# A decoder layer's MLP rows and last product: another order, the sums of w_down at another place, other tile sizes

## The chip, the cores and the metric

The kernel runs on one core of one Trainium2 chip. The metric is the device time in microseconds from the first to the last instruction of one execution, with what lies around it. Five engines work side by side, each on a queue of its own in a fixed order: PE (matmuls), ACT and DVE (elementwise work), POOL (a little elementwise work, and the issue of transfers), SP (the issue of transfers only). All transfers, whichever queue issues them, are carried out by the same 16 DMA engines.

## The reference

One decoder layer on 1024 tokens of width 1024, all in float32:

```python
n = rms_norm(h, ln_mix_g);  proj = n @ w_in
ya = dilated_mixture(qa, ka, va) @ w_branch_a        # 12 heads, three dilations
yb = stick_breaking(qb, kb, vb) @ w_branch_b         # 8 heads, causal
h  = h + (sigmoid(ga) * ya + sigmoid(gb) * yb) @ w_out
h  = h + memory_cross_attn(rms_norm(h), rms_norm(mem), ...)
u  = rms_norm(h, ln_ffn_g) @ w_up                    # 1024 -> 2 * 2816
u  = depthwise_conv(u, conv_w, width=3) + conv_b
h  = h + (silu(gate) * val) @ w_down                 # 2816 -> 1024
return rms_norm(h, ln_f_g)
```

What matters below are the last three lines: w_up with the convolution and the gate, w_down, and the final norm.

## The kernel before

**Products.** A float32 operand is split into a high part and the remainder (`split_to`, L82 on ACT and L83 on DVE), and every product is three matmuls of 128 x 512, high by high, high by low, low by high (`mm3`, L99 to L101).

**w_up.** The 44 column blocks of w_up are handled as 22 rows g, a gate block and a value block at a time. A row is a fast 2 x 2 block product: seven block products instead of eight, on sums of weight halves (`sum_weights`) and sums of activation halves (the tiles t2, t3, t4 of `right_sums`). A row accumulates in two PSUM banks. Bank A takes the product p1, then s2·t2 (copied out as U2, L948), then s1·t1 (copied out as U4, L953), then s4·22 (copied to ug, L958). Bank B takes s3·t3 (copied to uv, L917; an accumulating DMA from POOL adds U4 to it, L918) and then l22·t4 (copied to uv, and another accumulating DMA adds U2). Then ACT and DVE do the convolution of ug and uv (L966 to L968), Silu and the product (L970, L973), and POOL stores the result and its block sums to `r_d` in DRAM (L976 to L990). Row g+1 starts (`up_start`) ahead of the end of row g (`up_end`), and its middle (`up_middle`) behind it.

**Early rows.** For the rows g below NEARLY = 10 two of the seven products (p1 and the one that goes to ug) are made earlier, beside the cross attention (`up_early`), and parked in DRAM. p1 is parked as two halves phi and plo in `er_d`. In the row both halves are read back by DMAs from POOL's queue and put into bank A by two matmuls with the identity `ident_r` (L906, L907).

**w_down.** `down` makes seven products (`run`), each over 11 steps kg, one left operand for each product: four are blocks of w_down itself, three are sums of its blocks. These sums (`weight_sums`) are made in DRAM, in `sd_d`, without any engine: for each of the 11 kg, four plain DMAs from SP ("puts", L519, 256 KB each) and three accumulating DMAs from POOL ("adds", L522, one of 512 KB and two of 256 KB), each of which waits for the one before. `sum_step` issues what is due of them. It is called in the loop over the attention's units once p has reached the stick-breaking pairs, and eight times in the merge after it. Each call issues the next operation of every second sum or so.

**The end.** The last product's four tiles end together in the last kg. `into` adds them to h and squares them, and only then `out_half` scales the four tiles and stores them (L1035 to L1039). The loads of h for the first product (`load_h`) are issued at kg 3 to 6.

**Order and memory.** A scheduler fixes one order for each engine when the program is built. DMAs of the sums and of h keep their order in the code. SBUF tiles lie in pools that are stacked from the left and from the right. By the sizes of the tiles the left pools' rows begin at 128 bytes beyond a multiple of 256, those of most right pools (attention, cross attention, t2 to t4, w_down) at a multiple of 256.

## Time and profile before

| | us |
|---|---|
| three runs | 1784.14, 1780.95, 1777.82 |
| median | 1780.95 |
| profiled execution, whole | 1780.45 |
| profiled execution, span of the trace | 1778.6 |
| PE busy | 1693.4 (95%) |
| DVE busy | 1113.0 (63%) |
| ACT busy | 871.0 (49%) |
| POOL busy | 326.9 (18%) |

The stages in the span: projections to about 100 us, dilated attention to 400, stick-breaking attention to 740, merge to 822, w_out and cross attention to 1108, the early products and the sums of the activations to 1150, the 22 rows of w_up to 1530, the first product of w_down to 1585, six more of 30 us each, and a tail of 13 us behind the last matmul. A stage is read from its own rows: PE is busy nearly everywhere, so what counts is where it waits, and for whom.

### The profile page before, as it was taken

The page shows a single profiled execution, that of the slowest core. Times are in us where ns is not written, and L with a number is a line of the kernel's source. Part 1 is how long each engine was busy: PE and PEld are TensorE (multiplying, and loading weights), DVE is VectorE, ACT ScalarE, POOL GpSimd, SP SyncE. Part 2 cuts the span into 40 slices and gives each one's busy share as a digit, 9 for nine tenths or more (in the row PEclk, how much of TensorE's full clock was granted, in tenths as well). Part 3 has the DMA queues.
Part 4 walks back from the last instruction along what each step waited for, and adds up shares of the span by engine and source line. Part 5 has one row for each costly group of instructions (what it writes and reads, how often), then busy time and mean ns, then how long its engine had stood idle before and what let it go on. Part 6 is the DMA issues. An engine that isn't in the chain of part 4 may idle for free.

```text
span 1778.6 us, 23614 instructions
## 1 busy us (share of the span) xinstructions
PE 1693.4 (95%) x8598; PEld 1378.1 (77%) x8598; DVE 1113.0 (63%) x1737; ACT 871.0 (49%) x1495; POOL 326.9 (18%) x511
## 2 busy tenths in 40 slices
PE   7999999998999899999999989798999999989997
PEld 5977777878878787788888767576778888778885
DVE  3764654468757466575645666777777767655556
ACT  5344544466345445444534455454555555534344
POOL 0442333221112110001000102222222222200002
PEclk9999999999999999999999999899999999999999
DMA  7443333455774843566322325666755454677664
GB/s 305 113 123 92 107 83 84 134 134 145 200 140 118 159 113 95 180 181 249 131 95 72 130 83 178 206 165 184 211 148 157 136 136 125 188 259 231 214 191 140
DMA packets 106388, 273.01 MB, mean 153 GB/s; under 512 B 16096, under 2 KB 16352, under 8 KB 106272
## 3 DMA queue, kind: packets, MB, share of 16 engines
q1 hardware_dynamic: 66368, 166.68, 28.9%
q0 software_dynamic: 39904, 104.82, 24.1%
q8 instruction: 68, 1.11, 0.3%
q14 instruction: 48, 0.39, 0.1%
HBM read 188.77 MB, written 74.29 MB: 148 GB/s over the span
## 4 chain that ended last, share of the span: by engine, by line
PE 66%; issue 13%; DMA 10%; DVE 5%; ACT 3%; POOL 3%; SPq 0%; POOLq 0%; DVEq 0%; ACTq 0%
PE mm L99 4%; PE mm L101 4%; PE mm L100 4%; PE pA L99 3%; PE pA L100 3%; PE pA L101 3%; DMA sd_d<-in_w_down_dram 2%; DMA uv<-U 2%; PE mmt L99 2%; PE dA L100 2%; PE dA L101 2%; PE mmt L100 2%; PE mmt L101 2%; PE dA L99 2%; DMA xw<-xs 2%
## 5 line engine op out<-in xcount | busy, mean ns | idle before, releaser
L101 PE MATMUL mm<-a2h,wl 128*128 128x512 f32 x592 | 235.2, 398 | 0.0
L99 PE MATMUL mm<-a2h,wh 128*128 128x512 f32 x592 | 234.7, 396 | 0.0
L100 PE MATMUL mm<-a2l,wh 128*128 128x512 f32 x592 | 234.5, 396 | 0.0
L83 DVE TENSOR_TENSOR wl<-wr,wh 128x1024 fp32r<-128x1024 f32 (+1 forms) x119 | 145.3, 1222 | 95.0 <-ACT wh L82 92.1
L82 ACT ACTIVATE wh<-wr 128x1024 fp32r<-128x1024 f32 (+1 forms) x119 | 124.0, 1043 | 132.6 <-PE mmt L101 29.2
L83 DVE TENSOR_TENSOR dl<-rl,dh 128x1024 fp32r<-128x1024 f32 x77 | 94.1, 1224 | 85.0 <-ACT dh L82 81.5
L82 ACT ACTIVATE dh<-rl 128x1024 fp32r<-128x1024 f32 x77 | 81.2, 1058 | 114.6 <-PE dA L101 41.2
L101 PEld LDWEIGHTS mm<-a2h,wl 128*128 128x128 f32 x592 | 112.4, 190 | 22.2 <-issue 1.0
L100 PEld LDWEIGHTS mm<-a2l,wh 128*128 128x128 f32 x592 | 112.3, 190 | 22.3 <-issue 0.9
L99 PEld LDWEIGHTS mm<-a2h,wh 128*128 128x128 f32 x592 | 112.5, 190 | 22.0 <-issue 0.9
L493 DVE TENSOR_TENSOR_SCAN kp<-kp 128x128 f32<-128x128 f32 (+7 forms) x64 | 86.8, 1356 | 29.4 <-ACT kp L490 29.1
L99 PE MATMUL pA<-a2h,mh 128*128 128x512 f32 x176 | 70.5, 400 | 14.9 <-ACT U L953 14.9
L502 ACT ACTIVATE at<-tra 128x512 f32<-128x512 f32 (+3 forms) x96 | 43.3, 489 | 76.9 <-PE tra L500 59.6
L112 POOL TENSOR_TENSOR ss<-ss,neghalf 128x1 f32<-128x1 f32 x24 | 23.3, 995 | 307.6 <-DVE ss L597 305.7
L490 ACT ACTIVATE kp<-zz,zsc 128x512 f32<-128x512 f32 (+3 forms) x96 | 55.6, 583 | 49.3 <-DVE zz L489 44.5
L381 ACT ACTIVATE sp<-sp,nm 128x128 f32<-128x128 f32 (+1 forms) x96 | 42.3, 442 | 72.6 <-DVE nm L379 72.5
L100 PE MATMUL dA<-dl,dh 128*128 128x512 f32 x176 | 70.1, 398 | 3.5 <-DVE dl L83 3.5
L101 PE MATMUL dA<-dh,dl 128*128 128x512 f32 x176 | 70.0, 397 | 0.0
L101 PE MATMUL pA<-a2h,ml 128*128 128x512 f32 x176 | 69.3, 394 | 0.0
L100 PE MATMUL pA<-a2l,mh 128*128 128x512 f32 x176 | 69.3, 394 | 0.0
L99 PE MATMUL dA<-dh 128*128 128x512 f32 x176 | 62.1, 393 | 3.8 <-ACT dh L82 3.8
L491 ACT ACTIVATE gg<-zz,zsc 128x512 f32<-128x512 f32 (+3 forms) x96 | 55.7, 583 | 7.1 <-DVE gg L494 7.1
(352 smaller groups left out, 4587.4 us busy)
## 6 DMA issues: line engine op xcount, KB each, us to landing
rl<-r_d SPq DMA_DIRECT2D x77, 256.0 KB, 3.2
wr<-in_w_in_dram SPq DMA_DIRECT2D x37, 512.0 KB, 4.2
wr<-in_w_up_dram SPq DMA_DIRECT2D x32, 512.0 KB, 4.3
w<-in_w_up_dram SPq DMA_DIRECT2D x22, 512.0 KB, 3.7
uv<-U POOLq DMA_DIRECT2D x44, 256.0 KB, 4.7
r_d<-ts POOLq DMA_DIRECT2D x44, 256.0 KB, 4.8
rl<-sd_d SPq DMA_DIRECT2D x44, 256.0 KB, 3.6
r_d<-y POOLq DMA_DIRECT2D x33, 256.0 KB, 3.4
```

Of the source, the lines that this page charges most:

```text
L82: nc.scalar.activation(hi, raw, AF.Copy)
L83: nc.vector.tensor_tensor(lo, raw, f(hi), op=ALU.subtract)
L99: nc.tensor.matmul(ps, wh, rh, start=first, stop=False, **kw)
L100: nc.tensor.matmul(ps, wh, ro, start=False, stop=False, **kw)
L101: nc.tensor.matmul(ps, wo, rh, start=False, stop=last, **kw)
L112: nc.gpsimd.tensor_tensor(ss, ss, neghalf[:, :n], op=ALU.pow)
L381: nc.scalar.activation(sp[:, a, :n], sp[:, a, :n], AF.Exp, scale=0.125, bias=nm[:, a:a + 1], accum_out=ost[:, 130 + a:131 + a])
L490: nc.scalar.activation(kp[:, c0:c1], z[:, :n], AF.Sigmoid, scale=zsc[:, 1, i:i + 1])
L491: nc.scalar.activation(gg[:, c0:c1], z[:, :n], AF.Sigmoid, scale=zsc[:, 0, i:i + 1])
L493: nc.vector.tensor_tensor_scan(rev, rev, rev, 1.0, op0=ALU.mult, op1=ALU.bypass)
L502: nc.scalar.activation(s[:, :nb * P], tp[:, :nb * P], AF.Copy)
```

## The change

Six things change.

1. In the rows below 9 `up_end` writes l22·t4 ahead of s4·22.
2. p1 is parked as one float32 tile, stored from POOL, read back by SP, and put into bank A by one float32 matmul with `ident`. The subtraction that made plo, `er_d` and `ident_r` are gone.
3. Four tiles get other sizes, so that all pools begin at 128 bytes beyond a multiple of 256.
4. The sums of w_down leave the attention and the merge. `sum_step` is called twice in each row from g = 6 on, a sum's six operations follow each other step by step, and a new sum begins every second step. So from row 8 to row 16 one row issues four puts and three adds.
5. The loads of h stand at kg 6 to 9.
6. In the last product the last four kg are made tile by tile, and each tile is scaled and stored as soon as it is added.

```diff
-            if p >= NA:
-                sum_step()
...
-        sum_step()
...
     def sum_step():
-            d = n - 3 * b
-            if 0 <= d < 12 and d % 2 == 0:
-                ops[d // 2]()
+            d = n - 2 * b
+            if 0 <= d < 6:
+                ops[d]()
...
-    neghalf = cp.tile([P, 16], F32, name="neghalf")
-    ident_r = cp.tile([P, P + 16], F32R, name="ident_r")[:, :P]
+    neghalf = cp.tile([P, 32], F32, name="neghalf")
-    rs8 = ap.tile([P, 16], F32, name="rs8")[:, 0:8]
+    rs8 = ap.tile([P, 48], F32, name="rs8")[:, 0:8]
-        rsm = xp.tile([P, 18], F32, name="rsm")[:, :2]
+        rsm = xp.tile([P, 50], F32, name="rsm")[:, :2]
-    ncw = mp.tile([P, 160], F32, name="ncw")
+    ncw = mp.tile([P, 192], F32, name="ncw")
...
     def up_early(gs):
-            hi, lo = etile("phi", F32R), etile("plo", F32R)
-            hilo(hi, lo, ps[g][0])
-            nc.gpsimd.dma_start(er_d[g, 0], hi)
-            nc.gpsimd.dma_start(er_d[g, 1], lo)
+            p1 = etile("p1")
+            nc.scalar.activation(p1, ps[g][0], AF.Copy)
+            nc.gpsimd.dma_start(e_d[g, 0], p1)
...
     def up_start(g):
-            nc.gpsimd.dma_start(hi, er_d[g, 0])
-            nc.gpsimd.dma_start(lo, er_d[g, 1])
-            nc.tensor.matmul(u["A"], ident_r, hi, start=True, stop=False, skip_group_check=True)
-            nc.tensor.matmul(u["A"], ident_r, lo, start=False, stop=True, skip_group_check=True)
+            p1 = etile("p1")
+            nc.sync.dma_start(p1, e_d[g, 0])
+            nc.tensor.matmul(u["A"], ident, p1, start=True, stop=True, skip_group_check=True)
...
     def up_middle(g, u):
+        if g >= 6:
+            sum_step()
     def up_end(g, u):
+        if g >= 6:
+            sum_step()
+        for part in (c21, c12) if g + 1 < NEARLY else (c12, c21):
+            part()
...
     def run(ps, i, first, also=(), ends=0):
-                if kg >= 3 and kg - 3 < len(also):
-                    tc.keep_in_program_order(also[kg - 3]())
+                if kg >= 6 and kg - 6 < len(also):
+                    tc.keep_in_program_order(also[kg - 6]())
...
+            ws = [(kg, *operands(i, kg)) for kg in range(KG - ends, KG)]
+            for t in range(4 if ends else 0):
+                for w in ws:
+                    step(t, *w)
     def into(ps, th, ch, op, last=None):
+                if last:
+                    out_tile(4 * th + t)
...
-        out_half(0)
-        run(A, 3, False)
+        run(A, 3, False, ends=4)
         into(A, 1, 0, ALU.add, 1)
-        out_half(1)
```

`operands` is the loads and the split of one kg, `step` the three matmuls of one tile, and `out_tile` the body of the loop of `out_half`; they are taken out of their functions unchanged.

PE's order is nearly the same up to the early products. Of the places where orders differ, these follow. In the names, mh and ml hold the two halves of a pair of weight sums, wh and wl those of a weight block, a2h and a2l those of the activations.

PE before, row 1 of w_up: the last three matmuls of s1·t1 in bank A, and behind them the first three of s4·22 in the same bank.

```order
L99 MATMUL pA_10261<-a2h_9759,mh_10321 128x512
L100 MATMUL pA_10261<-a2l_9760,mh_10321 128x512
L101 MATMUL pA_10261<-a2h_9759,ml_10322 128x512
L99 MATMUL pA_10261<-a2h_9759,mh_10325 128x512
L100 MATMUL pA_10261<-a2l_9760,mh_10325 128x512
L101 MATMUL pA_10261<-a2h_9759,ml_10326 128x512
```

After, PE in the same row: behind the last three of s1·t1 stand the matmuls of l22·t4 in bank B, twelve in all.

```order
L97 MATMUL pA_10148<-a2h_9673,mh_10205 128x512
L98 MATMUL pA_10148<-a2l_9674,mh_10205 128x512
L99 MATMUL pA_10148<-a2h_9673,ml_10206 128x512
L97 MATMUL pB_10227<-t4h_10036,wh_10197 128x512
L98 MATMUL pB_10227<-t4l_10037,wh_10197 128x512
L99 MATMUL pB_10227<-t4h_10036,wl_10198 128x512
```

So twelve matmuls now stand between the two products of bank A. It is the same in rows 0, 2, 3 and 6. In row 4 of after (and in rows 5, 7 and 8) PE still has both products back to back, and l22·t4 comes after the next row has begun.

```order
L99 MATMUL pA_10491<-a2h_9673,ml_10562 128x512
L97 MATMUL pA_10491<-a2h_9673,mh_10561 128x512
L98 MATMUL pA_10491<-a2l_9674,mh_10561 128x512
L99 MATMUL pA_10491<-a2h_9673,ml_10562 128x512
L97 MATMUL pA_10491<-a2h_9673,mh_10565 128x512
L98 MATMUL pA_10491<-a2l_9674,mh_10565 128x512
L99 MATMUL pA_10491<-a2h_9673,ml_10566 128x512
```

The first of s4·22 is the last line there: nothing moved. In rows 11 and 13, which had 22 and 20 matmuls between the two products, there is none left after.

POOL before, a late row (U2, U4 and p1 are added to uv and ug; ts and y go to `r_d`): the additions of U4 and U2 stand one behind the other.

```order
L938 MEMSET uv_11911 128x2
L918 DMA ug_11910<-p1_11933 128x512
L980 DMA r_d_75<-y_11967 128x512
L981 DMA r_d_75<-y_11967 128x512
L986 DMA r_d_75<-ts_11975 128x512
L988 DMA r_d_75<-ts_11976 128x512
L990 DMA r_d_75<-ts_11977 128x512
L918 DMA uv_11911<-U4_12058 128x512
L918 DMA uv_11911<-U2_12031 128x512
```

POOL after, a late row: behind the addition of U4 stand the three adds of the sums, then two stores, then the addition of U2.

```order
L931 MEMSET uv_11977 128x2
L909 DMA uv_11977<-U4_12118 128x512
L519 DMA sd_d_73<-in_w_down_dram 128x512 x2
L519 DMA sd_d_73<-in_w_down_dram 128x1024
L977 DMA r_d_74<-y_12036 128x512
L985 DMA r_d_74<-ts_12189 128x512
L909 DMA uv_11977<-U2_12091 128x512
L931 MEMSET ug_12122 128x2
L909 DMA ug_12122<-p1_12145 128x512
```

The adds moved in between the two additions to uv, on the queue that carries both.

SP before, late rows: only the loads of the weights.

```order
L901 DMA w2_12358<-in_w_up_dram 128x1024
L72 DMA wr_12204<-in_w_up_dram 128x1024
L901 DMA w2_12497<-in_w_up_dram 128x1024
L72 DMA wr_12356<-in_w_up_dram 128x1024
L901 DMA w2_12649<-in_w_up_dram 128x1024
```

SP after, late rows: the same loads with four puts for each row among them.

```order
L894 DMA w2_12430<-in_w_up_dram 128x1024
L516 DMA sd_d_73<-sd_d_73 128x512
L516 DMA sd_d_73<-in_w_down_dram 128x512 x2
L70 DMA wr_12284<-in_w_up_dram 128x1024
L894 DMA w2_12585<-in_w_up_dram 128x1024
L516 DMA sd_d_73<-sd_d_73 128x512 x2
L516 DMA sd_d_73<-in_w_down_dram 128x512 x2
L70 DMA wr_12428<-in_w_up_dram 128x1024
L516 DMA sd_d_73<-sd_d_73 128x512
L894 DMA w2_12725<-in_w_up_dram 128x1024
```

The puts moved in ahead of the weights of the rows to come, and those that read `sd_d` wait for the adds.

## Rows read from the trace of the kernel before

**Rows 1.** page, part 1: busy us (share of the span) xinstructions

```profile
PE 1693.4 (95%) x8598; PEld 1378.1 (77%) x8598; DVE 1113.0 (63%) x1737; ACT 871.0 (49%) x1495; POOL 326.9 (18%) x511
```

**Rows 2.** busy time by stage of the end, columns in the first line

```profile
core 0: us, PE busy (x) PEld busy (x) DVE busy (x) ACT busy (x) POOL busy (x), PEclk, DMA share, GB/s
1108.00:1150.00 42.00, 32.09 (x123) 24.48 (x122) 34.70 (x38) 21.53 (x28) 10.38 (x21) 0.87 0.69 213
1173.00:1253.00 80.00, 70.57 (x295) 55.78 (x294) 61.11 (x67) 41.99 (x55) 24.57 (x48) 0.98 0.69 199
1309.30:1463.70 154.40, 154.40 (x672) 125.97 (x671) 117.12 (x122) 86.46 (x113) 37.34 (x68) 1.00 0.53 142
1530.00:1586.00 56.00, 48.65 (x198) 38.10 (x196) 32.96 (x32) 25.25 (x28) 7.19 (x13) 0.94 0.81 258
```

**Rows 3.** timeline of PE, row 1 and row 3: start, us, instruction, [idle before]

```profile
1174.89 0.50 PE L99 MATMUL pA<-a2h,mh 128*128 128x512 f32 x1 [1.41 <-ACT U L953]
...
1207.55 0.50 PE L99 MATMUL pA<-a2h,mh 128*128 128x512 f32 x1 [2.05 <-ACT U L953]
```

**Rows 4.** waits: who waited for whom: us in total, times, longest

```profile
PE pA L99 <- ACT U L953: 14.9, 8, 3.2
...
SPq L519 <- DMA sd_d<-in_w_down_dram: 157.0, 20, 21.1
...
ACT y L966 <- DMA uv<-U: 35.1, 18, 3.9
```

**Rows 5.** timeline of PE, transposes and attention values, float32

```profile
563.22 1.03 PE L500 MATMUL tra<-ident,gg 128*128 128x128 f32 x8
...
568.58 1.96 PE L507 MATMUL avs<-at,v 128*64 128x128 f32 x30
```

**Rows 6.** timeline of PE, early products

```profile
1121.01 0.80 PE L101 MATMUL pe<-a2h,wl 128*128 128x512 f32 x1 [5.55 <-DVE wl L83]
```

**Rows 7.** timeline of PE, a late row, first of twelve each

```profile
1389.29 0.40 PE L99 MATMUL pB<-t4h,wh 128*128 128x512 f32 x1
...
1392.08 0.39 PE L99 MATMUL pA<-a2h,mh 128*128 128x512 f32 x1
...
1394.82 0.40 PE L99 MATMUL pA<-t2h,mh 128*128 128x512 f32 x1
```

**Rows 8.** timelines of POOL, ACT and PE, stick-breaking attention

```profile
572.11 3.44 POOL L522 DMA_DIRECT2D sd_d<-in_w_down_dram  x4
...
609.86 2.86 POOL L522 DMA_DIRECT2D sd_d<-in_w_down_dram  x3
...
614.91 0.28 ACT L502 ACTIVATE at<-tra 128x128 f32<-128x128 f32 x1 [9.94 <-DMA yt_d<-ye]
...
615.24 0.69 PE L507 MATMUL avs<-at,v 128*64 128x128 f32 x2 [4.96 <-ACT at L502]
```

**Rows 9.** busy time in stretches of the stick-breaking attention, columns as above

```profile
488.30:492.00 3.70, 3.70 (x19) 3.03 (x18) 3.08 (x4) 2.32 (x7) 1.80 (x4) 1.00 0.61 171
572.00:592.00 20.00, 20.00 (x113) 15.85 (x112) 11.32 (x16) 10.88 (x22) 4.99 (x7) 1.00 1.00 176
600.00:620.00 20.00, 15.04 (x76) 11.91 (x75) 6.53 (x9) 5.02 (x11) 4.50 (x6) 0.83 0.80 167
614.90:624.60 9.70, 9.36 (x36) 7.30 (x37) 5.35 (x6) 6.18 (x12) 0.00 (x0) 0.74 0.77 123
```

**Rows 10.** DMA issues: count, KB each, median us from issue to landing

```profile
uv<-U POOLq DMA_DIRECT2D x44, 256.0 KB, 4.7
...
sd_d<-in_w_down_dram POOLq DMA_DIRECT2D x11, 512.0 KB, 9.9
...
sd_d<-in_w_down_dram POOLq DMA_DIRECT2D x22, 256.0 KB, 7.2
```

**Rows 11.** timeline of ACT, first product of w_down

```profile
1563.38 1.06 ACT L82 ACTIVATE dh<-rl 128x1024 fp32r<-128x1024 f32 x1 [3.38 <-DMA rl<-in_w_down_dram]
```

**Rows 12.** timeline of DVE, behind the last product

```profile
1763.60 1.37 DVE L1027 TENSOR_TENSOR h<-h,dA 128x512 f32<-128x512 f32 x2 [6.55 <-PE dA L101]
```

More of the change, by code (lines that the diff above doesn't have):

```diff
@@ L939, in up_middle @@
         if g < NEARLY:
[L940 removed]
+            nc.sync.dma_start(u["ug"][:, 2:2 + HT], e_d[g, 1])
         else:
@@ L1004, in load_h, with operands @@
             return [lambda t=t: nc.sync.dma_start(h[t][:, hs], h_d[t][:, hs]) for t in range(4 * th, 4 * th + 4)]
-        def run(ps, i, first, also=()):
-            for kg in range(KG):
-                if i == 1 and kg < 6:
-                    where = (bp, "wr", 2), (bp, "wh", 2), (bp, "wl", 2)
-                else:
-                    where = (dn, "rl", 6), *(((dn, "dh", 2), (dn, "dl", 2)) if kg % 2 else ((mp, "mh", 2), (mp, "ml", 2)))
-                raw, hi, lo = (pool.tile([P, 2, HT], d, tag=tag, name=n_, bufs=b) for (pool, tag, b), n_, d in
-                               zip(where, ("rl", "dh", "dl"), (F32, F32R, F32R)))
-                nc.sync.dma_start(raw[:, 0], r_d[kg, i - 1])
-                nc.sync.dma_start(raw[:, 1], left[i - 1](kg))
-                split_to(hi, lo, raw)
-                if kg >= 3 and kg - 3 < len(also):
-                    tc.keep_in_program_order(also[kg - 3]())
-                for t in range(4):
-                    ts_ = slice(t * P, (t + 1) * P)
-                    mm3(ps[t], (hi[:, 0, ts_], lo[:, 0, ts_]), (hi[:, 1], lo[:, 1]), first and kg == 0, kg == KG - 1,
-                        skip_group_check=True)
+        def operands(i, kg):
+            if i == 1 and kg < 6:
+                where = (bp, "wr", 2), (bp, "wh", 2), (bp, "wl", 2)
+            else:
+                where = (dn, "rl", 6), *(((dn, "dh", 2), (dn, "dl", 2)) if kg % 2 else ((mp, "mh", 2), (mp, "ml", 2)))
+            raw, hi, lo = (pool.tile([P, 2, HT], d, tag=tag, name=n_, bufs=b) for (pool, tag, b), n_, d in
+                           zip(where, ("rl", "dh", "dl"), (F32, F32R, F32R)))
+            nc.sync.dma_start(raw[:, 0], r_d[kg, i - 1])
+            nc.sync.dma_start(raw[:, 1], left[i - 1](kg))
+            return split_to(hi, lo, raw)
@@ new lines, in run, with step @@
+        def run(ps, i, first, also=(), ends=0):
+            def step(t, kg, hi, lo):
+                ts_ = slice(t * P, (t + 1) * P)
+                mm3(ps[t], (hi[:, 0, ts_], lo[:, 0, ts_]), (hi[:, 1], lo[:, 1]), first and kg == 0, kg == KG - 1,
+                    skip_group_check=True)
+            for kg in range(KG - ends):
+                w = operands(i, kg)
+                if kg >= 6 and kg - 6 < len(also):
+                    tc.keep_in_program_order(also[kg - 6]())
+                for t in range(4):
+                    step(t, kg, *w)
+            ws = [(kg, *operands(i, kg)) for kg in range(KG - ends, KG)]
+            for t in range(4 if ends else 0):
+                for w in ws:
+                    step(t, *w)
```

37 lines of the change are left out of this document (18 added, 19 removed).

## The prediction

> **What bounds the kernel now.** The sum is made against the profiled execution of 1780.45 us (span 1778.6), which lies 0.5 us under the median of 1780.95. I read the page first: PE is busy 95% of the span [rows 1], so only PE's waits and the speed of its matmuls can move the time. Then I read busy time by stage [rows 2]. In the late rows of w_up PE is busy 154.4 us of 154.4, with nothing to win but a faster matmul. In the early rows it lacks 9.4 us of 80, in the stage ahead of them 9.9 of 42, in the first product of w_down 7.4 of 56. The last column but one of the same rows is the share of time that the 16 DMA engines are busy: 0.53 in the late rows. The list of waits names the causes [rows 4]: PE waits 14.9 us in eight early rows for the copy U4.
>
> **The change part by part.**
>
> *Order in the early rows.* A row waits 1.41 us (row 1), 2.05 us (row 3) [rows 3], 14.9 in all over rows 1 to 8 [rows 4], about 0.16 more each for restarting. By PE's new order only rows 1, 2, 3 and 6 get twelve matmuls, 12 x 0.23 = 2.8 us [rows 7], between s1·t1 and s4·22, enough for these waits: 1.41 + 1.41 + 2.05 + 1.41 + 4 x 0.16 = 6.9 us to win. Rows 4, 5, 7 and 8 keep theirs. What is late next is uv: l22·t4 now follows s3·t3 by 12 matmuls instead of 24, and its copy to uv waits until the convolution of the row before has read uv, for which ACT already waits 18 times for the DMA (35.1 us in all) [rows 4]. I take -4 (0 to -7). Rows 11 and 13 lose their 22 and 20 matmuls of cover: up to two waits of 1.6 us, +3.2. I take 0, because these rows turn out to wait for transfers anyway (below), and keep both ends.
>
> *One float32 matmul for two.* Two matmuls of 512 columns at 0.23 us go, 0.46 us. No row shows a float32 matmul of full width that is not a transpose. Eight transposes of 128 columns take 1.03 us, 0.13 each, which is 0.52 for 512 columns. Thirty matmuls of 128 columns with 64 columns of weights take 1.96 us, 0.065 each [rows 5]: if they ran one by one, twice the weights cost 0.13 per 128 columns, again 0.52; if two of them ran side by side, one took 0.13 and twice the weights 0.26, 1.04 for 512. Between 0.52 and 1.04 I take the middle, 0.78, so +0.32 a row, since nothing tells the two apart. For the six rows ahead of the sums that is +2 (from -2.3, if it costs no more than one of the old matmuls, to +5.8, ten rows at 0.58). The ten subtractions of plo leave DVE in the stage from 1108 to 1150, where DVE is busy 34.7 of 42 us and PE waits 5.55 us for it once [rows 2, 6]. Ten subtractions at about 0.7 us, as the 0.68 each of the pair of like size at the end [rows 12], are 7 us of DVE; I take -3 for PE (0 to -6). Behind p1's load on SP stand the weights of the next rows. It waits for a store made some 50 us earlier, so I cost it at nothing; if it were late, a row would wait up to a transfer, 4.7 us [rows 10].
>
> *256-byte steps.* Twelve matmuls of pB<-t4,wh, whose operands begin 0 and 128 bytes beyond a multiple of 256, take 1392.08 - 1389.29 = 2.79 us; twelve of pA<-a2h,mh, both at 128, take 2.74 [rows 7]: 4 ns each. Some 1,460 matmuls mix the two: 36 in each of 22 rows of w_up, and some 670 in the gates, w_out and the attention. That is 6 us if this is the cause; less what falls into rows that wait for transfers, I take -4 (0 to -7).
>
> *The sums leave the attention.* At 609.86 POOL issues three adds; PE then waits 4.96 us for a copy on ACT that had waited 9.94 us for the DMA yt_d, which stands behind adds in POOL's queue [rows 8]. From 600 to 620 PE is busy 15.04 of 20 us, and the granted clock is 0.83 on average [rows 9]: 1.2 instead of 2.4 GHz for 0.17 x 2 x 20 = 6.8 us, about half of them idle, so 3.4 us of work took twice its time and cost 1.7. With the wait that is 6.7. I take -7 (0 to -9, for smaller waits).
>
> *The sums in w_up.* This is the largest term. First the price in DMA time. Three adds, 1 MB, fill 0.77 x 9.7 = 7.5 us with one put among them; from 572 to 592 the engines are busy 20 us of 20 with four adds (1.5 MB), 0.5 MB of stores, part of another add and two puts [rows 8, 9]. So 1 MB of adds costs 6.5 to 9 us of all 16 engines; I take 7.8, between the two. Three puts fill 0.61 x 3.7 = 2.3 us [rows 9], four 3.0. A sum is 10.8 us (9 to 13). Then the room. A late row has 154.4 / 8 = 19.3 us, of which transfers fill 0.53, 10.2 us; an early row 0.69 x 16 = 11.0 [rows 2], less one 256 KB read. One sum per row makes 21.0 us of transfers in 19.3 in rows 10 to 16 (+1.7 x 7 = 12), 20.8 in row 8, which lasted 16 (+4.8), 20.8 in 19.3 in row 9 (+1.5), and 18.1 in 16 in row 7 with three quarters of one (+2.1). Sum +20.4. The highest share that held for 20 us is 1.00 [rows 9], so I let nothing overlap. Part of the backlog costs nothing: uv may land about 10 us later than it does before U4 of the next row (46 matmuls lie between l22·t4 and that copy in the new order) is held up on ACT behind the convolution. 20 - 10 = +10. Ends: 0 if a sum costs 9; +41 at 13 without any tolerance. What is queued behind: on POOL, the adds wait for puts, and the addition of U2 and the stores to r_d wait behind them; on SP, puts wait for adds (157 us of such waits in the old place [rows 4]), and the weights of the next row stand behind.
>
> *h later, and the end.* At the first product ACT waits 3.38 us for a weight load, among loads of h [rows 11]. In SP's new order the first h stands one pair of loads away from its old place: -0.5 (0 to -2). At the end DVE begins at 1763.60 [rows 12], 2.0 us ahead of PE's last end. With the last 12 matmuls belonging to one tile it can begin about 1.2 us earlier: -1.2 (0 to -1.5).
>
> *Sum.* Order -4, injection +2, DVE's relief -3, padding -4, attention -7, sums +10, h -0.5, end -1.2: -7.7, and 1780.45 - 7.7 = 1773.
>
> **The rivals.**
>
> *A: the sums fit in.* If packets of two queues overlap on an engine, a busy share of 1.00 is no ceiling, and the 9.1 us that a late row leaves free hold more than they seem. For it: from 572 to 592, at share 1.00, only 176 GB/s move, while 1530 to 1586 moves 258 at 0.81 [rows 2, 9]. Against it: the adds that came together there landed late. Without the +10 the time is 1780.45 - 17.7 = 1763. The Trainium skill, "Perfetto Trace Analysis", section "Identifying the Most-Contended Engine", calls occupancy misleading for the 16 DMA engines and wants HBM utilization read instead; by that rule the 142 GB/s of a late row leave room, and this rival would be the forecast. No row here shows an add beside w_up's transfers.
>
> *B: the sums hold up the rows (slower).* From 9.1 us per sum on, each row lasts as long as its transfers, and with the upper price of 13 that is 23.2 us for rows 10 to 16. The queues make it worse: adds wait for puts and puts for adds, 9.9 us for the large add and 7.2 for a small one [rows 10] in a loop that must close within a row. +41 in place of +10 gives 1804. For it: SP waited 157 us for such adds before [rows 4]. Against it: the 10 us of tolerance.
>
> *C: the early rows and the padding bring nothing.* uv takes the place of U4 and the 4 ns have another cause: +8, 1781. For it: in rows 4, 5, 7 and 8 the change does not do what it says. Against it: the 2.8 us of cover in four rows are plain in the order.
>
> The Trainium skill, "FP8 and Floating Point Precision", section "TensorE Precision Notes", gives a true float32 product four passes. By that the injection would take 4 x 0.23 = 0.92 us, and its term would be 6 x 0.46 = +2.8 instead of +2; by the transposes it would be about 0. No row decides it.
>
> **How the numbers follow.** The forecast has 0.42 (its own range 1765 to 1782, from the ends of the smaller terms), A 0.20, B 0.23, C 0.15. Leaving out a tenth at either side, the range is 1758 to 1802. A measurement of this kernel can tell about 0.3%, 5.3 us, from no change. Faster by more: two thirds of the forecast's 0.42 and nearly all of A, 0.48. Slower by more: nearly all of B and a little of the rest, 0.26. Within: 0.26.
>
> **What would show it.** Order: waits of PE for U4 in rows 4, 5, 7 and 8 alone, and no new idle time of ACT ahead of the convolution. Injection: 0.78 us from the float32 matmul to the next one. Padding: 12 matmuls of pB<-t4 in 2.74 us. Attention: no wait near 4.96 us for yt_d, clock 1.00 from 600 to 620. Sums: DMA share of rows 8 to 16 near 1.00 and rows of 20 to 21 us; at 19.3 us A holds, at 22 and more B. End: DVE's first addition 3 us or more ahead of PE's last end. The forecast is wrong if a sum costs the 16 engines clearly less than 9 us or more than 12.

## The result and the profile after

The changed kernel takes 1808.4 us (median of four, 1803.1 to 1811.8) against 1779.7 us: a ratio of 1.0155, interval 1.0122 to 1.0189. It is 28.8 us slower, 35 us over the forecast of 1773 and 6 us beyond the end of the range at 1802. The direction was that of rival B. The profiled execution took 1810.15 us, span 1808.3, which is 29.7 us more than that of before.

Page of after, part 1, answers to [rows 1]: PE's busy time went up by 8 us and the span by 30, so most of the loss is waiting.

```profile
PE 1701.3 (94%) x8598; PEld 1379.9 (76%) x8598; DVE 1106.4 (61%) x1727; ACT 870.2 (48%) x1494; POOL 308.4 (17%) x481
```

Busy time by stage of after, columns as in [rows 2]. The first four lines answer to [rows 2] (the last of them is the first product of w_down, which moved), the fifth to the third line of [rows 9]. The windows of the first two lines are the same times as before, but the work has moved ahead in them, by 10 to 18 us: the first one now holds the first row of w_up.

```profile
1108.00:1150.00 42.00, 36.69 (x153) 28.04 (x152) 30.34 (x33) 19.98 (x27) 6.00 (x12) 1.00 0.59 180
1173.00:1253.00 80.00, 72.28 (x290) 56.05 (x289) 59.53 (x66) 39.54 (x50) 20.78 (x38) 0.96 0.68 191
1309.30:1463.70 154.40, 133.45 (x538) 104.85 (x537) 96.57 (x102) 71.27 (x94) 49.47 (x78) 0.94 0.83 194
1564.00:1617.00 53.00, 46.66 (x191) 37.06 (x190) 31.95 (x30) 24.78 (x27) 7.44 (x13) 0.94 0.82 261
600.00:620.00 20.00, 20.00 (x112) 16.05 (x111) 11.91 (x13) 9.79 (x19) 0.53 (x1) 1.00 0.15 53
```

Read the third line first. In the late rows, where PE had been busy all the time with 672 matmuls, it now does 538 in the same 154.4 us and idles 21 of them. DMA share is 0.83: the engines are not full. Elsewhere things got better: the attention between 600 and 620 has no gap and full clock, and from the first early product to the first row of w_up PE lacks 15.0 us of 116.2 instead of 19.6 of 124.1.

Where the 29.7 us come from is read from the time at which the same matmul starts in both timelines. The first column says from which to which.

| stretch | before, us | after, us | difference |
|---|---|---|---|
| start to the merge behind the attention | 750.5 | 742.4 | -8.2 |
| merge to the early products | 273.9 | 272.0 | -2.0 |
| early products, to the first row of w_up | 124.1 | 116.2 | -7.9 |
| rows 0 to 4, and what is moved of row 5 | 81.1 | 76.0 | -5.2 |
| rows 5 to 21 | 301.0 | 358.0 | +57.0 |
| w_down | 234.5 | 232.4 | -2.2 |
| last matmul to the end | 13.4 | 11.5 | -1.9 |

Everything up to row 5 gains 23 us, and the rows that hold the sums lose 57. One profiled execution each stands behind this table, and stretches of the same code differ by some us between executions (below, at the old code order).

Waits of after from 1225 to 1530, who waited for whom: us in total, times, longest.

```profile
ACT y L967 <- DMA uv<-U: 63.6, 13, 9.1
...
ACT uv L908 <- DVE y L969: 26.0, 11, 5.1
...
PE pA L97 <- ACT U L946: 21.7, 7, 7.9
```

ACT's convolution of uv (line 967) waits for the transfer that adds U2 to uv, 4.9 us each time. Behind it on ACT stand the copies that empty PE's banks, so PE waits for ACT. ACT's 63.6 us are not themselves the loss; PE's 21.7 us behind them are a part of it.

The chain of after (the work that ended last, followed back from the end) from 1365 to 1420: start, us, what. The transfers uv<-U are its longest pieces: the one of 9.13 us here and one of 12.28 us that starts at 1415.49. Over the whole run the additions of U2 in rows 6 to 11 and 13 to 16 are on the chain.

```profile
1371.52 9.13 DMA uv<-U
1380.67 1.25 ACT y L967
1382.00 1.29 DVE y L968
1383.32 1.30 DVE y L969
1384.64 1.24 DVE y L974
...
1387.80 0.61 DVE wl L81
1388.43 0.70 DVE w L917
...
1390.12 1.05 ACT wh L80
1391.22 0.50 PE pA L97
```

One row's chain: U2's addition takes 9.13 us, then come the convolution on ACT and three steps on DVE, then the split of the next weights that stood behind them on DVE and ACT, then PE. What the transfer queued behind is in the timeline of POOL: start, us, instruction.

```profile
1361.95 0.85 POOL L909 DMA_DIRECT2D uv<-U  x1 [0.70 <-ACT uv L908]
1362.49 2.87 POOL L519 DMA_DIRECT2D sd_d<-in_w_down_dram  x3
1364.09 1.85 POOL L977 DMA_DIRECT2D r_d<-y  x1
1364.67 1.82 POOL L985 DMA_DIRECT2D r_d<-ts  x1
...
1371.52 0.89 POOL L909 DMA_DIRECT2D uv<-U  x1 [1.52 <-ACT uv L908]
```

U4's addition, three adds of the sums, two stores, and then U2's addition. In the trace the three adds land at 1369.8, 1372.9 and 1376.7, the stores at 1378.1 and 1379.0, and U2's addition at 1380.65: in the order of issue. So do all 395 transfers of POOL's queue in this trace.

### The profile page after: what moved, and what is told of

The parts are those of the page before. It is cut to its first block, busy times and chain, and to the rows that moved or that the text cites. A ratio compares the mean times of both kernels' runs of the same rounds, so it can differ in the third digit from the quotient of the medians.

```text
span 1808.3 us, 23552 instructions
## 1 busy us (share of the span) xinstructions
PE 1701.3 (94%) x8598; PEld 1379.9 (76%) x8598; DVE 1106.4 (61%) x1727; ACT 870.2 (48%) x1494; POOL 308.4 (17%) x481
## 4 chain that ended last, share of the span: by engine, by line
PE 53%; DMA 15%; issue 13%; DVE 9%; ACT 6%; POOL 3%; SPq 0%; POOLq 0%; DVEq 0%; ACTq 0%
DMA uv<-U 7%; PE mm L97 4%; PE mm L99 4%; PE mm L98 4%; DMA xw<-xs 3%; PE mmt L97 2%; PE mmt L98 2%; PE dA L98 2%; PE dA L99 2%; PE dA L97 2%; PE mmt L99 2%; PE pA L97 2%; PE dB L98 2%; PE dB L97 2%; PE dB L99 2%
## 5 line engine op out<-in xcount | busy, mean ns | idle before, releaser
L81 DVE TENSOR_TENSOR wl<-wr,wh 128x1024 fp32r<-128x1024 f32 (+1 forms) x119 | 145.4, 1223 | 96.1 <-ACT wh L80 91.9
L80 ACT ACTIVATE wh<-wr 128x1024 fp32r<-128x1024 f32 (+1 forms) x119 | 124.1, 1044 | 134.9 <-PE mmt L99 28.3
L81 DVE TENSOR_TENSOR dl<-rl,dh 128x1024 fp32r<-128x1024 f32 x77 | 94.1, 1225 | 82.6 <-ACT dh L80 82.2
L97 PE MATMUL pA<-a2h,mh 128*128 128x512 f32 x176 | 74.3, 422 | 26.1 <-ACT U L946 26.1
L968 DVE SCALAR_TENSOR_TENSOR y<-uv,ncw,y 128x1024 f32<-128x1024 f32 x22 | 28.3, 1284 | 91.5 <-ACT y L967 91.4
L487 ACT ACTIVATE kp<-zz,zsc 128x512 f32<-128x512 f32 (+3 forms) x96 | 55.7, 584 | 49.0 <-DVE zz L486 44.2
L98 PE MATMUL pA<-a2l,mh 128*128 128x512 f32 x176 | 73.3, 417 | 0.0
```

The source lines that it names most:

```text
L80: nc.scalar.activation(hi, raw, AF.Copy)
L81: nc.vector.tensor_tensor(lo, raw, f(hi), op=ALU.subtract)
L97: nc.tensor.matmul(ps, wh, rh, start=first, stop=False, **kw)
L98: nc.tensor.matmul(ps, wh, ro, start=False, stop=False, **kw)
L487: nc.scalar.activation(kp[:, c0:c1], z[:, :n], AF.Sigmoid, scale=zsc[:, 1, i:i + 1])
L968: nc.vector.scalar_tensor_tensor(y, x_[:, 1:1 + T], cw[:, c0 + 1:c0 + 2], y, op0=ALU.mult, op1=ALU.add)
```

## The experiments

Times are medians; "before" is the kernel before on the same chip, 1780.8 to 1782.9 us. Each edit is against the changed kernel unless it says otherwise.

**The sums back in the attention.** The steps go back to their old places and spacing; all else stays changed.

```diff
-            d = n - 2 * b
-            if 0 <= d < 6:
-                ops[d]()
+            d = n - 3 * b
+            if 0 <= d < 12 and d % 2 == 0:
+                ops[d // 2]()
...
+            if p >= NA:
+                sum_step()
...
-        if g >= 6:
-            sum_step()
...
```

> The changed kernel with the sums of w_down back in their old place (the attention's loop and the merge, with the old pacing); the five other parts stay. Theory S (the sums stretch the rows of w_up): in the trace of the change the start of row 5 lies 23 us earlier than before and the first product of w_down 34 us later, so the sums cost about 57 us there and won about 8 in the attention: 1808 - 57 + 8 = about 1759, and the late rows last 19.0 to 19.3 us again. Rival O (the new orders in the rows, the float32 injection or the new tile places stretch the rows): the late rows stay at 22 us or more, 1795 to 1815.

1769.3 us, ratio 0.9933 (0.991 to 0.9955). The move of the sums alone turned a gain of 11.6 us into a loss of 28.8. The wait in the attention is back, in the timeline of PE of this kernel:

```profile
615.66 0.69 PE L504 MATMUL avs<-at,v 128*64 128x128 f32 x2 [4.36 <-ACT at L499]
```

**Only the sums moved.** The kernel before, with the sums at the changed kernel's places.

```diff
-            d = n - 3 * b
-            if 0 <= d < 12 and d % 2 == 0:
-                ops[d // 2]()
+            d = n - 2 * b
+            if 0 <= d < 6:
+                ops[d]()
...
-            if p >= NA:
-                sum_step()
...
+        if g >= 6:
+            sum_step()
...
```

> The kernel before with the sums of w_down moved into the rows of w_up, and nothing else. Theory S: 1780 - 8 + 57 = about 1829 (1815 to 1840), late rows of 22 to 26 us. Rival O: 1770 to 1780, late rows of 19.3 us.

1830.3 us, ratio 1.0282 (1.0232 to 1.0333): 49.5 us lost without any other part of the change, as expected from 57 lost in the rows and 8 won in the attention. Its chain from 1340 to 1400, the additions of U2 alone, alternates between rows; the one at 1350.48 was issued behind the adds of line 522.

```profile
1349.95 0.53 POOL sd_d L522
1350.48 16.84 DMA uv<-U
...
1378.75 7.66 DMA uv<-U
...
1398.39 15.45 DMA uv<-U
```

**No sums at all.** The changed kernel without any step of the sums; w_down reads blocks of the weights instead of `sd_d`, so its output is another and only its time is of use.

```diff
-        if g >= 6:
-            sum_step()
...
-        left = [lambda kg: w_down[0, kg][:, :HT], lambda kg: w_down[0, kg][:, HT:], lambda kg: sd_d[kg][:, 3],
+        left = [lambda kg: w_down[0, kg][:, :HT], lambda kg: w_down[0, kg][:, HT:], lambda kg: w_down[1, kg][:, :HT],
...
```

> The changed kernel without the sums of w_down: no DMA of theirs is issued, and w_down's products read blocks of w_down in their place, so that the output is another. Theory S: about 1750 (1745 to 1756), which is what the other five parts give, 30 us less than before. Rival O: 1795 or more.

1753.5 us, ratio 0.9851 (0.9803 to 0.9899). So the sums in w_up cost 1808.4 - 1753.5 = 55 us, and all the rest of the change, with the sums' absence from the attention, brings 27 us. The kernel with the sums back differs from this one in the sums alone (and in the blocks that w_down reads): in their old place they cost 1769.3 - 1753.5 = 15.8 us.

**The second step of a row later.** It moves from the start of `up_end` to behind its products, so that it is issued after U2's addition.

```diff
     def up_end(g, u):
-        if g >= 6:
-            sum_step()
...
         for part in (c21, c12) if g + 1 < NEARLY else (c12, c21):
             part()
+        if g >= 6:
+            sum_step()
```

> The changed kernel with the second step of the sums written at the end of up_end's products instead of at its start: on POOL's queue the three adds then stand behind the addition of U2 to uv, and the additions of U4 and U2 stand one behind the other as before. The DMA work of a row stays the same, 21 to 23 us of the 16 engines by the rows of before. Theory F (the place in POOL's queue: the addition of U2 lands 9 to 12 us after its issue because adds and stores stand ahead of it): rows of 19.3 to 20.5 us from 8 to 16, 1760 to 1775. Theory C (the work of the 16 DMA engines, or the loop of puts and adds, sets a row's length): rows stay at 21.5 us or more, 1790 to 1810.

1768.4 us, ratio 0.9933 (0.9915 to 0.9951): 40 of the 55 us come back, with the same sums in the same rows. Busy time from 1300 to 1460 in this kernel and, in the second line, with no sums, columns as before:

```profile
1300.00:1460.00 160.00, 153.49 (x671) 125.07 (x670) 114.00 (x120) 84.72 (x112) 57.70 (x92) 1.00 0.96 238
1300.00:1460.00 160.00, 160.00 (x707) 132.54 (x706) 121.99 (x127) 91.05 (x118) 38.41 (x70) 1.00 0.53 143
```

The DMA share is higher than in the slow kernel, 0.96 against 0.83. So the engines being full is not what cost the 40 us; the place in POOL's queue is. (The step's puts on SP moved with its adds. DVE waits 4.7 us for weights that SP loads in after, from 1225 to 1530, and 2.1 us here, so SP's part is small.) From 1225 to 1530 ACT still waits 53.6 us for U2's additions, against 63.6, but PE's waits for copies of U fall from 21.7 to 7.9 us. With 84 matmuls to a row, the two lines give 20.0 us for a row here and 19.0 without sums, and additions of U2 on the chain land 8 us after they are issued:

```profile
1362.82 7.95 DMA uv<-U
...
1382.18 8.58 DMA uv<-U
...
1403.27 8.16 DMA uv<-U
```

**The sums thinner.** The kernel of the last experiment, with sums three steps apart, from row 4 on.

```diff
-            d = n - 2 * b
+            d = n - 3 * b
...
-        if g >= 6:
+        if g >= 4:
```

> As adds_late (the adds behind the addition of U2), and thinned out: the steps begin at row 4 and a new sum begins every third step, so that a row has two thirds of a sum, about 6 us of DMA work in place of 9, from row 4 to row 21. Theory W (in adds_late the late rows last 20.0 us in place of 19.04 because the 16 engines are busy 0.96 of the time): at two thirds the share is about 0.85, the late rows return to 19.0 to 19.2 us, early rows gain nothing, 1755 to 1762. Rival L (a row's loop of puts and adds, not the work, stretches the rows of adds_late): rows stay at 19.7 us or more and there are five more of them, 1768 to 1775.

1770.6 us, ratio 0.9935 (0.991 to 0.9961). That is in the rival's range, but not for its reason: the late rows are back at 19.04 us, and PE at full work:

```profile
1300.00:1460.00 160.00, 159.86 (x706) 132.09 (x705) 121.82 (x126) 90.51 (x118) 55.33 (x89) 1.00 0.88 215
```

The gain is lost in rows 6 and 8, where additions of U2 on the chain take 11.69 and 10.94 us: an early row is shorter, which would leave such a wait less room. The first product of w_down is longer too, 57.0 us instead of 52.2. Together with no sums (19.0 us at share 0.53) and adds late (20.0 at 0.96), this says that a share of 0.88 costs nothing by itself, and that at 0.96 a row lost 1.0 us.

**The loop through uv.** From these traces the size of the loss can be worked out. For rows 9 to 19 the table has the mean time from issue to landing of U2's addition, the mean time from one row's issue to the next, and their difference.

| kernel | U2 lands after, us | row, us | rest, us |
|---|---|---|---|
| before | 4.2 | 19.1 | 14.8 |
| no sums | 4.5 | 19.0 | 14.5 |
| sums thin | 6.5 | 19.1 | 12.6 |
| adds late | 6.9 | 19.5 | 12.6 |
| after | 9.0 | 22.0 | 13.0 |
| only the sums moved | 10.4 | 23.1 | 12.6 |

The rest is what has to follow between the landing in one row and the next row's issue. The chain of after shows it closing in more than one way, through the fixed orders of ACT's and DVE's queues as well as through the buffer of uv. In row 11 (above) convolution and DVE's steps hold up the split of the next weights, and these PE. In row 7 the copy of U4, which stands behind the convolution on ACT, holds up PE, and after 36 matmuls and the copy to uv the next U2 is issued. In the four kernels with sums in the rows the mean of the rest is 12.6 to 13.0 us; in the single rows 9 to 16 of after it lies between 10.4 and 15.6. So the estimate, from these means, is that a row of 19.04 us has room for a landing of some 6.5 us, and that beyond it each us of landing is about a us of row. It holds for means and not row by row: with sums thin the addition of row 14 lands after 8.6 us, and its row still lasts 19.0.

**Padding alone.** The kernel before with the three padded tiles.

```diff
-    rs8 = ap.tile([P, 16], F32, name="rs8")[:, 0:8]
+    rs8 = ap.tile([P, 48], F32, name="rs8")[:, 0:8]
...
-        rsm = xp.tile([P, 18], F32, name="rsm")[:, :2]
+        rsm = xp.tile([P, 50], F32, name="rsm")[:, :2]
...
-    ncw = mp.tile([P, 160], F32, name="ncw")
+    ncw = mp.tile([P, 192], F32, name="ncw")
```

> The kernel before with the three tile sizes of the right pools changed and nothing else, so that all pools begin at 128 bytes beyond a multiple of 256. Theory P (operands at different places modulo 256 cost 4 to 10 ns a matmul): matmuls of pB<-t4 and of mmt<-wh,o at 227 ns in place of 231 and 232, late rows of 19.04 in place of 19.35 us, in all 6 to 8 us less, 1772 to 1775 against 1780. Rival: the gain of those matmuls in the changed kernel came from elsewhere, and nothing changes.

1769.3 us, ratio 0.9929 (0.9899 to 0.996), a gain of 7 to 18 us by that interval. The stretch of the third line of [rows 2] now holds 683 matmuls instead of 672:

```profile
1309.30:1463.70 154.40, 154.40 (x683) 127.85 (x682) 118.65 (x124) 88.56 (x116) 39.03 (x69) 1.00 0.54 148
```

By starts in the late rows, 48 of the 84 matmuls took 229 to 234 ns before, by the mean of each product and operand, and all take 227 now. A late row lasts 19.04 us instead of 19.35. By landmarks the profiled execution gains 14.6 us: 3.2 ahead of the rows, 8.5 in them (5.0 in rows 0 to 9, where stretches at half the clock, 1.2 GHz, between 1142 and 1152 are gone as well), 2.9 in w_down.

**Adds late with the old code order in the rows.**

```diff
-        for part in (c21, c12) if g + 1 < NEARLY else (c12, c21):
+        for part in (c12, c21):
```

> adds_late with the old order of the last two products in all rows (s4·22 ahead of l22·t4). Theory U (in rows 1 to 5 the new order wins 4 to 5 us, in rows 6 to 9 it loses as much, because l22·t4 then waits for uv): rows 0 to 5 take 79 us in place of 75, the whole within 3 us of 1768. Rival G (the new order is a gain of 4 to 7 us as I forecast): 1772 to 1776.

1767.6 us, ratio 0.9919 (0.9891 to 0.9948), the same as adds late (1768.4). The reason is in the order of the instructions: with either line of code all five engines run the same instructions in the same order, in the rows and everywhere else. The edit of the order moves nothing: the two kernels are one program, measured twice.

**Adds late with the old injection.** The two rounded parts, stored and loaded on POOL's queue, and two matmuls; `up_early` goes back with it.

```diff
-            p1 = etile("p1")
-            nc.sync.dma_start(p1, e_d[g, 0])
-            nc.tensor.matmul(u["A"], ident, p1, start=True, stop=True, skip_group_check=True)
+            hi, lo = etile("phi", F32R), etile("plo", F32R)
+            nc.gpsimd.dma_start(hi, er_d[g, 0])
+            nc.gpsimd.dma_start(lo, er_d[g, 1])
+            nc.tensor.matmul(u["A"], ident_r, hi, start=True, stop=False, skip_group_check=True)
+            nc.tensor.matmul(u["A"], ident_r, lo, start=False, stop=True, skip_group_check=True)
...
```

> adds_late with the old injection of p1 (two halves through DRAM, two matmuls, loads on POOL's queue). By the trace of the change the float32 matmul costs 0.85 us from its start to the second matmul behind it less one, against 0.46 for the two, so ten rows get 3.9 us back; but the stage of the early products, which lasted 18 us less up to its end in the change than before, 8 us of them in the stage itself, loses these 8 us with the subtractions. Theory D (DVE's relief is the larger part): the first t2 matmul comes 7 to 9 us later than in adds_late, and the whole is 4 to 8 us slower, 1772 to 1777. Rival: the stage gained by something else, and the whole is 3 to 4 us faster, 1764.

1782.2 us, ratio 1.0013 (0.9989 to 1.0037), 14 us more than adds late. Its profiled execution, at 1776.8 us one of its fastest, shows 10.5 of them. In it the stage of the early products is 6.3 us longer and rows 0 to 9 are 5.2 us longer, with 18.4, 16.9 and 19.6 us in rows 3 to 5, ahead of any sum, where padding alone has 15.8, 15.8 and 17.3.

**Padding and the float32 injection,** in the kernel before, with its old code order; the injection's lines are the reverse of the last diff.

> The kernel before with the new tile places and the float32 injection of p1. With the tile places alone it took 1769. Theory D (the injection relieves DVE by ten subtractions and POOL's queue by thirty transfers): the stage of the early products ends 6 to 8 us sooner against its own start, rows 0 to 9 cost 4 us more on PE and win some of it back, 1762 to 1766. Rival: the rows lose what the stage wins, 1768 to 1771.

1773.0 us, ratio 0.9943 (0.9923 to 0.9964), 3.7 us over padding alone, which ran on another chip; the intervals of the two ratios overlap, so a loss is not shown. The expected gain did not come. The stage ahead of the rows is 4.5 us shorter, as it was to be, but from the start of row 0 to that of row 9 it takes 148.3 us instead of 143.6, and the first product of w_down 55.7 instead of 52.3. (Its profiled execution also loses 5.9 us up to the merge, far from the rows, of which 1.4 are made up before the early products, so one profile does not place the 3.7 us well.) Why the rows do not gain is in PE's order: with this edit alone, in the old code order, l22·t4 stands between the two products of bank A in rows 1, 2, 3, 6 and 8, as it does in the first four of these with the change. The scheduler moved it because of the injection. Timeline of PE, padding with injection, row 6:

```profile
1252.61 0.55 PE L97 MATMUL pB<-t4h,wh 128*128 128x512 f32 x1 [3.53 <-ACT uv L911]
```

and one of the waits of padding alone in these rows, row 5:

```profile
1234.56 0.50 PE L99 MATMUL pA<-a2h,mh 128*128 128x512 f32 x1 [2.96 <-ACT U L953]
```

The wait for U4 has become one for the copy to uv.

**The sums back, old code order.**

```diff
-        for part in (c21, c12) if g + 1 < NEARLY else (c12, c21):
+        for part in (c12, c21):
```

> sums_back (all of the change but the sums' place, 1769) with the old order of the last two products. Theory N (the new order brings nothing, since l22·t4 waits for uv in place of s4·22 for U4, and the longer waits of rows 6 to 8 drop the clock): 1764 to 1769. Rival G (the new order is worth 4 us, as I forecast): 1772 to 1775.

1771.5 us, ratio 0.9947 (0.993 to 0.9965), between the two expectations and within the interval of the sums back with the new order. Again all five engines run the same instructions in the same order with either line, so the new line of code is worth nothing. The two pairs of one program say what small differences mean here: their medians lie 0.8 and 2.2 us apart, and in this pair's profiled executions the first product of w_down takes 52.0 and 55.0 us.

**Five sums in the attention, six in the late rows.** The code order is the old one.

```diff
+        for b, ops in enumerate(sums[:5]):
+            d = n - 6 * b
+            if 0 <= d < 12 and d % 2 == 0:
+                ops[d // 2]()
...
+        for b, ops in enumerate(sums[5:]):
+            d = n - 4 * b
...
+        if g >= 9:
+            row_step()
```

> Sums of w_down at half the density in two places: five of the eleven in the attention with a new one every sixth call in place of every third, six in rows 9 to 21 of w_up with a new one every second row and their adds behind the addition of U2. Old order of the last two products in all rows; float32 injection, tile places, later h and the end as in the change. Theory W (the sums cost time where they pile up: behind POOL's waiting adds in the attention, and at a DMA share of 0.96 in the rows): share 0.75 to 0.8 in the late rows, rows of 19.04 us, no wait near 5 us at yt_d; 3 to 6 us over the 1753 without sums, 1756 to 1760. Rival (what costs is that there are sums at all, 55, 15 or 16 us for eleven, in proportion): about 15 over, 1768.

1766.2 us, ratio 0.9913 (0.9892 to 0.9933), the lowest median here of a kernel that computes the whole reference, by less than such a difference, and short of the 1756 to 1760 that I expected. In neither place does PE wait for the sums. Busy time in the attention and in the late rows:

```profile
600.00:620.00 20.00, 20.00 (x111) 16.05 (x110) 12.41 (x13) 9.55 (x21) 2.03 (x3) 1.00 0.69 111
1309.00:1463.00 154.00, 154.00 (x681) 127.58 (x680) 117.11 (x122) 86.58 (x113) 48.57 (x80) 1.00 0.84 198
```

PE misses nothing in the late rows at a DMA share of 0.84, one hundredth above that of after, where it missed 21 us. What is late next is the first product of w_down, 57.9 us instead of 53.1. Waits from 1534 to 1560:

```profile
ACT dh L80 <- DMA rl<-in_w_down_dram: 11.0, 2, 7.6
...
PE dA L97 <- ACT dh L80: 6.1, 1, 6.1
```

SP reaches these loads late: a put of the last sum, which waits for an add, is issued at 1525.81, and the loads behind it from 1530.51 on. Rows 0 to 9 wait as before: PE 10.4 us for the copy to uv and 4.4 us for U4, together 14.8, where [rows 4] has 14.9 for U4 alone.

```profile
PE pB L97 <- ACT uv L919: 10.4, 5, 4.2
PE pA L97 <- ACT U L957: 4.2, 3, 1.4
PE pA L97 <- ACT U L952: 0.2, 1, 0.2
```

**The same with the old injection,** six sums in the attention, and five from row 10 on, three steps apart.

```diff
-        for b, ops in enumerate(sums[:5]):
+        for b, ops in enumerate(sums[:6]):
...
-            d = n - 4 * b
+            d = n - 3 * b
...
-        if g >= 9:
+        if g >= 10:
```

> The changed kernel with the rows in the old order, the old injection (two rounded parts, stored and loaded on POOL's queue, two matmuls with the identity), six of the eleven sums in the attention with six steps between their starts, and five sums in rows 10 to 20, three steps apart, each step at the end of the row's transfers. No row that loads the injection's parts on POOL's queue has a sum in it. Theory N (the old injection cost 14 us in the pair with all sums in the rows only because its loads stood behind the adds on POOL's queue; where no add is queued, it is the float32 one that costs more, as 1773.0 against 1769.3 had it): rows 0 to 9 last about 144 us instead of 152, the stage ahead of them some 4.5 us longer, no gap over 3 us in the attention: 1757 to 1763. Rival G (the old injection costs 10 us or more everywhere, by DVE's subtractions and POOL's loads): 1770 to 1776. Rival R (as N, but adds in the late rows stretch them again): rows 10 to 20 over 19.3 us, 1764 to 1769.

1769.4 us, ratio 0.9929 (0.9913 to 0.9946): no better. The parts came as the first theory had them (145.4 us instead of 152.2 from the start of row 0 to that of row 9, the early products 124.7 instead of 117.2, the first product of w_down 52.0 instead of 57.9), and rows 9 to 20, from start to start, lose 6 us, of which 2.9, 1.1 and 2.3 in rows 9, 10 and 15. So the injection moves time between stages and its balance is within a few us. The 14 us of the pair above are not a price of the old injection: that pair also differs in PE's order in the rows, and this one, in which the sums' spacing changed too, has no such gap. Which part of the 14 us belongs to the order and which to loads behind adds was not separated.

## Why the prediction failed, step by step

**The sums in w_up: +10 forecast, +55 measured.** This is the step that failed. Its price was right: with no sums a row of 19.0 us is filled to 0.53, 10.1 us; with adds late one of 20.0 us to 0.96, 19.2, so by this stretch a sum costs the engines 9.1 us. Over the whole traces they are busy 787 us with no sums and 903 in after, 10.6 us for each of eleven sums. I took 10.8 (9 to 13), so the sign that I had named for a wrong forecast, a price clearly below 9 or above 12, did not show, and the forecast failed all the same. What failed is the model around the price. I let a row last as long as its transfers, and then gave uv "about 10 us" of tolerance because 46 matmuls lie between l22·t4 and the next U4. Two things were wrong.

- The tolerance was counted in PE's order, not around the loop that has to close within a row. U2's addition, the convolution, DVE's steps, what stands behind them on ACT and DVE, PE's next products, and the next copy to uv follow one another, some 12.5 us without the landing. By that estimate the landing in a row of 19.04 us may grow from 4.2 us to about 6.5, by 2.3 us and not 10. And I took the backlog as one sum over all rows, to be set once against a tolerance; a wait in such a loop comes back in each row.
- The landing was not costed by its place in the queue. The order of POOL shown ahead of the prediction has three adds and two stores between U4's addition and U2's, and the text says that U2 waits behind them, but puts no number to it. The landings came to 9.1 to 15.0 us in rows 9 to 16. That they would be long was to be seen in rows of before: three adds one behind the other, at 7.2 and 9.9 us each [rows 10], with stores behind them.

In after landing and rest make 9.0 + 13.0 = 22.0 us for rows 9 to 19 against 19.04, 33 us in eleven rows. Another 22 us are in rows 6 to 8, with landings of 10.1, 11.6 and 9.7 us and 25.0, 27.4 and 23.4 us from issue to issue instead of 17.2, 16.4 and 20.3. Part of both is work at half the clock behind the stalls: from 1100 us on, 90 matmuls that start 0.43 us apart add 18 us to the same matmuls at 0.23; with adds late 29 of them add 6, with no sums 48 add 10.

The 9.1 us "from which each row lasts as long as its transfers" was no threshold either. Rival B had the place and the sign right. Its time of 1804 was near by luck, since it was worked out from engines that are full at 13 us a sum, and that was not what held the rows. Its second sentence, on the queues, came nearer; but the loop it names is that of adds and puts, not the one of U2.

**Rival A, and the share.** At a share of 0.83 and 194 GB/s the rows lost 21 of 154 us; at 0.84 and 198 GB/s, in the split, nothing; at 0.88 and 215 GB/s nothing; at 0.96 and 238 GB/s 1.0 us a row. Neither column forecasts the loss. The rule of the Trainium skill, "Perfetto Trace Analysis", section "Identifying the Most-Contended Engine", that occupancy misleads, agrees with the first three of these. Utilization, which it wants read in its place, does not tell the loss either: the lowest of these four rates, 194 GB/s, goes with the largest loss. What decides is when one particular transfer lands.

**Order: -4 forecast, 0 measured.** Two kernels with the old line of code run the same instructions in the same order as their partners with the new one. The order that I read from the changed kernel is there, but the injection makes the scheduler choose it, and it wins nothing: the uv copy takes the place of U4, 14.8 us (split) against 14.9. That was the first half of rival C. I had priced the gain by the waits removed and not by the one that is late next, though I named it.

**Injection and DVE's relief: +2 and -3 forecast.** The pieces went as described. Timeline of PE of after, first row:

```profile
1131.12 1.02 PE L898 MATMUL pA<-p,ident 128*128 128x512 f32 x2
1131.57 0.79 PE L97 MATMUL pA<-t2h,mh 128*128 128x512 f32 x1
1132.20 0.39 PE L98 MATMUL pA<-t2l,mh 128*128 128x512 f32 x1
```

From 1131.12 to 1132.20, less the 0.23 of one matmul, it costs 0.85 us, so 0.39 more than two old ones (forecast 0.32). By the four passes of the Trainium skill, "FP8 and Floating Point Precision", section "TensorE Precision Notes", the estimate was 0.92; the trace has 0.85, halfway between it and the 0.78 that I took, and records the float32 matmul as two. PE's wait of 5.55 us [rows 6] is gone (the longest for `wl` in that stage is 0.7 in after); the stage gains 4.5 us with the padding already in place, more than the 3 I took. What I left out is that the edit changes the order of the rows, which gives it back: no gain in padding with injection, 3.7 us more by the medians, within the noise.

**Padding: -4 forecast, -12 measured** (7 to 18). The 4 ns were about right (229 to 234 ns, now 227), but 48 matmuls of a row had them, not 36, and in the profiled executions waits and half-clock stretches in the rows and in w_down shrank with it. The second half of rival C falls.

**The attention: -7 forecast, about -16 measured.** The gap that I priced is gone: PE is busy all the time and at full clock from 600 to 620. But I priced that one gap and put the smaller waits, with a bound of -9, at next to nothing. Without the sums the kernel with the sums back gains 15.8 us. In the profiles the five kernels with all sums in the attention reach the merge at 749.3 to 755.3 us, seven with none there at 738.2 to 744.8, some 10 us sooner in the mean; where the rest of the 16 lies was not placed.

**h and the end: -0.5 and -1.2 forecast.** The first product of w_down lasts 53.1 us after, 52.3 with padding and the old h: later loads of h bring nothing that shows. At the end DVE begins at 1793.64, PE's last matmul at 1796.84; with its 0.39 us that is 3.6 us ahead of PE's end instead of 2.0, and the end is 1.9 us shorter.

```profile
1793.64 1.29 DVE L1038 TENSOR_TENSOR h<-h,dA 128x512 f32<-128x512 f32 x2 [4.94 <-PE dA L99]
```

Without the sums the other terms came to -27 us instead of -17.7: -15.8 from the attention and -11.6 from the five other parts (the sums back, against before). For these five I had forecast -10.7, but that this sum was near is luck: padding alone brought -12, and order, injection and h nothing that shows. The one step, sums in w_up, turned the sign.

**What stays open.** In the orders with the float32 injection rows 5 to 9 are longer than with the old one even where there is no sum, with waits of 3 us and half-clock stretches behind them; that the scheduler's order does it is seen, but not tried by fixing the order and changing the matmul alone. A second buffer for uv was not tried; since the chain also closes through ACT's and DVE's queues, it isn't shown that it would break the loop.

## What to carry to other kernels

Work that is "free" on the DMA engines is costed by the queue it is issued on: look for what is issued behind it on the same queue, and whether that transfer is part of a loop that must close in every row. The tolerance of such a loop is the row less the loop's other steps, here 19.0 - 12.5 = 6.5 us for a landing by the means; it is read around the loop, through every engine, and it does not add up over rows. Where a scheduler sets the order, ask which edit causes a move before its gain is booked to the line of the diff that talks of order: two kernels whose engines all run the same order are one program.

## What the runs showed of the hardware

- Transfers of one software queue landed in the order of issue here: none of POOL's 395 transfers in after landed ahead of one issued before it. An addition of 256 KB that took 4.2 us in rows 9 to 19 of before took 9.1 to 15.0 us behind three accumulating adds and stores, and up to 16.84 us in the kernel with only the sums moved. The DMA issues of after from 1310 to 1460 show it for the stores too (count, KB each, median us to landing); they took 3.9 (`ts`) and 3.2 us (`y`) in the same stretch of before.

```profile
r_d<-ts POOLq DMA_DIRECT2D x13, 256.0 KB, 10.9
...
r_d<-y POOLq DMA_DIRECT2D x10, 256.0 KB, 8.9
```

- With three tiles made longer, so that the tiles behind them start at other offsets, 48 of a row's 84 matmuls of 512 columns went from 229 to 234 ns to 227 ns.
- A 512-column float32 matmul cost 0.85 us, and the 16 engines held a busy share of 0.96 over 160 us while PE ran at full clock with 6.5 us of waits.
